# Value products one head later in a sparse-attention loop, its compressed branch behind the third head, and two tails in another order

## The chip, the cores and the metric

The kernel runs on one core of a Trainium2 chip. The metric is the time of one execution in device microseconds (us). TensorE is called PE in the rows (its weight loads PEld), VectorE DVE, ScalarE ACT, GpSimd POOL, and SyncE, which issues the transfers, SP.

## The reference

A trunk of two decoder layers on 256 tokens of width 1024, in float32. Each layer is a half feed-forward block, a token mixer and another half feed-forward block, each added to the residual. The mixer of layer 0 is native sparse attention, that of layer 1 differential attention.

```
for layer in range(2):
    x = x + 0.5 * swiglu(rmsnorm(x, ffn1_norm[layer]), ffn1_w_in[layer], ffn1_w_out[layer])
    hn = rmsnorm(x, mix_norm[layer])
    if layer == 0: y = nsa_mixer(hn, ...)
    else:          y = diff_mixer(hn, ...)
    x = x + y
    x = x + 0.5 * swiglu(rmsnorm(x, ffn2_norm[layer]), ffn2_w_in[layer], ffn2_w_out[layer])
```

Sparse attention has 16 query heads of 64 that share 4 key and value heads, and three branches: one over 15 compressed blocks, whose keys and values come out of a small MLP; one over selected blocks (with 256 tokens all that are causal); and one over a window.

```
o_cmp = softmax(q kc * scale - slope * dist) vc        # kc, vc = MLP of overlapping blocks
o_sel, o_win = the same over ks, vs and over kw, vw
o = g0 * o_cmp + g1 * o_sel + g2 * o_win               # g = sigmoid(gates), for each head
y = o @ w_out
```

Differential attention subtracts two softmaxes of each of 8 heads, multiplies by v, normalizes each head's output (subln) and projects it.

## The kernel before

Every product of full precision is made of three in a reduced one: weights and activations are split into a high and a low part (`whi`, `wlo`, `oh`, `ol`: ACT writes the high one, DVE subtracts it), and the products high by high, low by high and high by low are added up in one of eight PSUM banks, `B[0]` to `B[7]` (L383 to L385). The weights come in by DMA in an order fixed ahead and are split by L86 (ACT) and L89 (DVE).

The program's order on each engine is set by a scheduler out of the order in which the code issues, of the dependencies and of priorities: what stands inside `tc.high_priority` goes ahead of other work that is ready. Each engine then runs its own list in order. A piece of code that is written as a generator (`yield`) is advanced by its caller with `next` or finished with `run`.

Sparse attention (`nsa`) runs in these steps:

1. The projections. During the first (`q0`) and the one for v the generator `mlp` makes the compressed keys and values. Its last step, reached at `k == 4` of the v projection (`MLP_K`), turns the keys (transpose L748) and spreads the values (L750) in the bank `pk = B[4]`; ACT and DVE take them into `kcT` (L753, L754) and `vb` (L759).
2. `cmp_group(g, bank)`, the compressed branch for eight heads: 16 score products (L828), a softmax on DVE (L834 to L850, the exponential on ACT, L845), two transposes (L854) and the copy `pcT` (L855). For the first eight heads it is run before the loop, in `B[3]`; for the others it is part of the filler.
3. `head_loop` over 16 heads, written below. `qk(i)` are the scores (L894 and L897, high and low keys), `chain(i)` the softmax on DVE and ACT (L572, L573), the reciprocal and gating (L917, L918) and the scaling of the probabilities `p` (L921, L923), `tr(i)` six transposes (L930) and two copies `pT` (ACT L932, DVE L933). `pv(i)` does nothing for an even head; for an odd one it multiplies a pair's probabilities by the values: one product of the compressed branch (L942) and 16 half-height ones (L949), and then `oh` on ACT (L951) and `ol` on DVE (L952). Each pair of heads writes its half of `B[7]`.
4. `fill` advances the filler between the heads: the projection `q1` of the second eight heads, its transposes (`q_t`, L788, L791), the second `cmp_group`, and the part of the output projection (`out_proj`) for the pairs that are done. What is left of it is run behind the loop.

```
    def head_loop(n, qk, chain, tr, pv, fill, counts, pumps, mid=None, depth=1):
        for i in range(depth):
            qk(i)
            chain(i)
        if mid:
            mid(0)
        for i in range(n):
            with tc.high_priority(offset=0):
                tr(i)
                if i + depth < n:
                    qk(i + depth)
                    chain(i + depth)
            W.pump(pumps[i] // 10, 512)
            fill(counts[i])
            W.pump(pumps[i] % 10, 512)
            with tc.high_priority(offset=0):
                if mid and i + 1 < n:
                    mid(i + 1)
                pv(i)
```

The sparse loop calls it with a depth of 2 and no `mid`. `out_proj(half, 1, ...)` makes the second half of the heads for two of the four output banks: it yields after each bank's first products, and each bank's end is followed by the addition to the residual.

Differential attention ends with `sub_b(3, B[5])`, the normalization of the last two heads: a chain on DVE, four transposes (L1035), then `oh` on ACT (L1037) and `ol` on DVE (L1038), which the last products of each output bank need.

Of the kernel before, what the change touches and what calls it, by code (L numbers as in the profile page):

```python
# [25 lines left out]
HQ = 16  # L26
# [30 lines left out]
class Stream:  # L57
# [54 lines left out]
    def next(self, key):  # L112
        i = self.i
        assert self.chunks[i][0] == key, (self.chunks[i][0], key)
        while self.ns <= i:
            self._piece(2048)
        self.i += 1
        if self.eager:
            self.pump(99, 512)
        return self.split.pop(i)  # L120
# [3 lines left out]
def trunk_kernel(ctx, tc, x, ffn1_norm, ffn1_w_in, ffn1_w_out, mix_norm, ffn2_norm, ffn2_w_in, ffn2_w_out,  # L124
# [11 lines left out]
    B = [pp.tile([P, 512], F32, name=f"bank{i}") for i in range(8)]  # L136
# [438 lines left out]
    def out_proj(half, hg, oh, ol, nxt, scale):  # L575
        hi, lo = W.next("op%d%d" % (half, hg))
        hv, lv = halves(hi, 4), halves(lo, 4)
        for jp in range(2):
            for dd in range(4):
                d = half * 4 + dd  # L580
                for j in (2 * jp, 2 * jp + 1):
                    mm3(B[d // 2][:, (d % 2) * S:(d % 2 + 1) * S], hv[:, j, dd * P:(dd + 1) * P], lv[:, j, dd * P:(dd + 1) * P],
                        oh[:, 4 * hg + j, :], ol[:, 4 * hg + j, :], hg == 0 and j == 0 and d % 2 == 0, hg == 1 and j == 3)
                if hg == 1 and jp == 1 and d % 2:
                    residual_bank(d // 2, scale, nxt)
                if dd % 2:
                    yield

    def run(gen):
        for _ in gen:  # L590
            pass
# [10 lines left out]
                    self.live = False  # L602
                n -= 1

    def head_loop(n, qk, chain, tr, pv, fill, counts, pumps, mid=None, depth=1):
        for i in range(depth):
            qk(i)
            chain(i)
        if mid:
            mid(0)  # L610
        for i in range(n):
            with tc.high_priority(offset=0):
                tr(i)
                if i + depth < n:
                    qk(i + depth)
                    chain(i + depth)
            W.pump(pumps[i] // 10, 512)
            fill(counts[i])
            W.pump(pumps[i] % 10, 512)
            with tc.high_priority(offset=0):  # L620
                if mid and i + 1 < n:
                    mid(i + 1)
                pv(i)

    OWN_BANK = 5
    NSA_FILL = [7, 1, 1, 3, 0, 2, 2, 0, 0, 1, 0, 3, 0, 3, 0, 5]
    NSA_PUMP = [2, 42, 12, 42, 0, 24, 44, 40, 11, 42, 0, 4, 33, 3, 1, 40]
# [3 lines left out]
    NSA_POST = 0  # L631
    DIFF_POST = 0
    FFN_SPLIT = 0
    MLP_K = [0, 1, 4]
    QT_K = [1, 4, 5, 6]
    START_SPLIT = 0
    QRAW = 'svss'
# [5 lines left out]
    def nsa(nrm, nxt_g):  # L643
# [52 lines left out]
        def mlp():  # L696
            e2 = t2("e2", 64)
            nc.gpsimd.tensor_tensor(e2, ident[:, :64], ident[:, 64:], op=ALU.add)
            for kv in range(2):
                for half in range(2):  # L700
                    hi, lo = W.next("w1")
                    hv, lv = halves(hi, 8), halves(lo, 8)
                    for ii in range(8):
                        i = half * 8 + ii
# [37 lines left out]
            for g in range(2):  # L742
                for a in range(2):
                    c0 = (2 * g + a) * NCMP
                    nc.gpsimd.tensor_copy(halves(rr[:DH, g * P + a * DH:g * P + (a + 1) * DH], 4),
                                          ident[:DH, c0:c0 + NCMP].unsqueeze(1).to_broadcast([DH, 4, NCMP]))
            pk = B[4]
            nc.tensor.transpose(pk[:, :DH], ck[:DH], ident[:DH, :DH])  # L748
            for g in range(2):
                nc.tensor.matmul(pk[:, (1 + g) * DH:(2 + g) * DH], rr[:DH, g * P:(g + 1) * P], cc[:DH, DH:P],  # L750
# [12 lines left out]
        m = mlp()  # L763
# [44 lines left out]
        for tb in range(2):  # L808
            nc.scalar.activation(vn[:, tb, 0:256], B[2][:, tb * 256:(tb + 1) * 256], AF.Copy, scale=r[:, tb:tb + 1])
            nc.scalar.activation(vn[:, tb, 256:512], B[3 + 4 * tb][:, 0:256], AF.Copy, scale=r[:, tb:tb + 1])  # L810
        gv = gate.rearrange("p b (h c) -> p b h c", c=3)
        fcg = bp.tile([P, 2, HQ], F32, tag="fcg", name=nm("fcg"))
        oh = t8("oh", F32R).rearrange("p (k t) -> p k t", k=KT)
        ol = t8("ol", F32R).rearrange("p (k t) -> p k t", k=KT)
# [137 lines left out]
            nc.vector.tensor_tensor(ol[:, hp, :], b, oh[:, hp, :].bitcast(F32), op=ALU.subtract)  # L952

        gates()
        run(cmp_group(0, B[3]))
        fill = Fill(filler())
        W.eager = False
        W.pool = NSA_SPLIT
        head_loop(HQ, qk, chain, tr, pv, fill, NSA_FILL, NSA_PUMP, depth=2)
        W.eager = True  # L960
        W.pool = NSA_POST
        fill(1000)
        nxt = Norm(nxt_g)
        run(out_proj(0, 1, oh, ol, nxt, 1.0))
        run(out_proj(1, 1, oh, ol, nxt, 1.0))
        return nxt

    def diff(nrm, nxt_g):
# [5 lines left out]
        oh = t8("oh", F32R).rearrange("p (k t) -> p k t", k=KT)  # L974
# [67 lines left out]
        def pv(j, pt):  # L1042

            for h in (2 * j, 2 * j + 1):
                assert h in ready
                vs = slice(h * P, (h + 1) * P)
                a = (h % 2) * 256
                nc.tensor.matmul(pt[:, a:a + P], at[:, h % 5, :P], vt[:, 0, vs], start=True, stop=True, skip_group_check=True)
                for sb in range(2):
                    nc.tensor.matmul(pt[:, a + P:a + 2 * P], at[:, h % 5, (1 + sb) * P:(2 + sb) * P], vt[:, sb, vs],  # L1050
                                     start=sb == 0, stop=sb == 1, skip_group_check=True)
            raw = ob[j] = t2("oraw")
            nc.vector.tensor_copy(raw, pt)
# [126 lines left out]
        W.pool = TAIL_SPLIT  # L1180
        fill(1000)
        nxt = Norm(nxt_g)
        o1 = out_proj(0, 1, oh, ol, nxt, 1.0)
        next(o1)
        next(o1)
        W.pool = DIFF_POST
        run(s3)
        run(o1)
        run(out_proj(1, 1, oh, ol, nxt, 1.0))
        return nxt  # L1190

    W.pool = START_SPLIT
# [57 lines left out]
```

## Time and profile before

| | us |
|---|---|
| median of 3 runs | 1046.07 (1044.92 to 1046.37) |
| the profiled execution | 1046.42 |
| its span | 1044.6 |
| PE busy | 1027.9, 98% |
| DVE busy | 780.4, 75% |
| ACT busy | 621.1, 59% |
| POOL busy | 42.9, 4% |

The span is the time that the hardware profiler saw between the first and the last instruction of the core; the execution's time is that and what lies around it. Busy time is the sum over an engine's instructions of the time in which one was running; matmuls are pipelined, so two can overlap.

### The profile page before, as it was taken

What the parts mean: (1) busy time and instruction counts of PE and PEld (TensorE: products, weight loads), DVE (VectorE), ACT (ScalarE), POOL (GpSimd) and SP (SyncE); (2) the same over time, 40 slices, a digit from 0 to 9 for tenths busy, and PEclk for the clock granted to TensorE, in tenths of its full rate; (3) what the DMA queues carried; (4) which work ended last, traced back from release to release, by engine and by line L of the source; (5) the groups of instructions that cost most, each with busy time, mean ns of one, the idle gap of its engine ahead of it and who ended that gap; (6) DMA issues with size and microseconds to landing.
All of it is one profiled execution on the core that took longest, in us unless ns stands there. A gap on an engine that the chain in (4) does not pass through costs nothing.

```text
span 1044.6 us, 17571 instructions
## 1 busy us (share of the span) xinstructions
PE 1027.9 (98%) x6486; PEld 912.8 (87%) x6486; DVE 780.4 (75%) x1834; ACT 621.1 (59%) x1407; POOL 42.9 (4%) x86
## 2 busy tenths in 40 slices
PE   8999999999999999999999999999999999999998
PEld 7999999879777899999999999999878898888887
DVE  7775766889887795766679676667987988676674
ACT  6555555768677664555556555546677656556552
POOL 0000000000231100000000000000032000000000
PEclk9999999999999999999999999999999999999999
DMA  8656565478410256565555556565534335655541
GB/s 279 226 179 211 171 204 176 148 161 252 160 41 1 85 201 215 171 211 168 202 183 181 194 169 202 162 202 163 205 122 161 122 121 176 218 174 199 198 165 40
DMA packets 130482, 178.14 MB, mean 171 GB/s; under 512 B 5674, under 2 KB 105180, under 8 KB 130396
## 3 DMA queue, kind: packets, MB, share of 16 engines
q1 hardware_dynamic: 130220, 176.95, 52.3%
q8 instruction: 50, 0.82, 0.3%
q14 instruction: 36, 0.29, 0.1%
q10 hardware_dynamic: 176, 0.07, 0.0%
HBM read 175.96 MB, written 1.05 MB: 169 GB/s over the span
## 4 chain that ended last, share of the span: by engine, by line
PE 91%; DVE 4%; ACT 3%; issue 1%; DMA 1%; SPq 0%; POOL 0%; ACTq 0%; DVEq 0%; POOLq 0%
PE bank L420 28%; PE bank L422 15%; PE bank L383 7%; PE bank L385 7%; PE bank L384 7%; PE bank L388 6%; PE bank L389 6%; PE bank L390 6%; PE bank L949 2%; DVE wlo L89 2%; PE bank L930 1%; PE bank L897 1%; PE bank L1108 1%; ACT whi L86 1%; ACT p L573 1%
## 5 line engine op out<-in xcount | busy, mean ns | idle before, releaser
L89 DVE TENSOR_TENSOR wlo<-raw,whi 128x512 fp32r<-128x512 f32 x667 | 431.5, 683 | 136.0 <-ACT whi L86 134.6
L86 ACT CAST whi<-raw 128x512 fp32r<-128x512 f32 x667 | 373.5, 617 | 212.8 <-PE bank L420 126.3
L420 PE MATMUL bank<-xhl,whi 128*128 128x512 f32 x1280 | 450.8, 393 | 0.0
L422 PE MATMUL bank<-xhl,wlo 128*128 128x256 f32 x1280 | 361.7, 283 | 0.0
L420 PEld LDWEIGHTS bank<-xhl,whi 128*128 128x128 f32 x1280 | 240.5, 188 | 53.9
L422 PEld LDWEIGHTS bank<-xhl,wlo 128*128 128x128 f32 x1280 | 240.7, 188 | 0.4
L388 PE MATMUL bank<-hh,whi 128*128 128x256 f32 x528 | 149.4, 283 | 0.0
L389 PE MATMUL bank<-hh,wlo 128*128 128x256 f32 x528 | 149.3, 283 | 0.0
L390 PE MATMUL bank<-hl,whi 128*128 128x256 f32 x528 | 149.3, 283 | 0.0
L440 DVE TENSOR_TENSOR ab<-bank,sh 128x256 f32<-128x256 f32 x160 | 60.4, 418 | 73.7 <-ACT sh L439 73.7
L439 ACT COPY sh<-bank 128x256 f32<-128x256 f32 x160 | 55.9, 373 | 95.3 <-PE bank L422 95.1
L388 PEld LDWEIGHTS bank<-hh,whi 128*128 128x128 f32 x528 | 101.0, 191 | 1.2
L390 PEld LDWEIGHTS bank<-hl,whi 128*128 128x128 f32 x528 | 101.1, 191 | 0.0
L389 PEld LDWEIGHTS bank<-hh,wlo 128*128 128x128 f32 x528 | 101.0, 191 | 0.0
L383 PE MATMUL bank<-whi,xhl 128*128 128x512 f32 (+2 forms) x192 | 75.7, 394 | 0.0
L384 PE MATMUL bank<-wlo,xhl 128*128 128x512 f32 (+2 forms) x192 | 72.9, 380 | 0.7 <-DVE wlo L89 0.7
L385 PE MATMUL bank<-whi,xhl 128*128 128x512 f32 (+2 forms) x192 | 72.9, 380 | 0.0
L442 DVE TENSOR_TENSOR ab<-ab,rb 128x512 f32<-128x512 f32 x80 | 54.6, 683 | 0.0
L573 ACT ACTIVATE p<-p,mn 128x128 f32<-128x128 f32 (+1 forms) x96 | 43.1, 452 | 11.9 <-DVE mn L572 11.5
L448 ACT CAST hh<-sh 128x256 fp32r<-128x256 f32 x88 | 34.8, 399 | 19.4 <-DVE sh L446 19.4
L384 PEld LDWEIGHTS bank<-wlo,xhl 128*128 128x128 f32 x192 | 36.2, 189 | 6.9 <-DVE wlo L89 1.1
L385 PEld LDWEIGHTS bank<-whi,xhl 128*128 128x128 f32 x192 | 36.1, 188 | 6.7
(259 smaller groups left out, 1331.0 us busy)
## 6 DMA issues: line engine op xcount, KB each, us to landing
raw<-in_ffn_w_in_dram SPq DMA_DIRECT2D x174, 512.0 KB, 5.0
raw<-in_ffn_w_out_dram SPq DMA_DIRECT2D x44, 1024.0 KB, 5.0
raw<-in_diff_w_in_dram SPq DMA_DIRECT2D x12, 1024.0 KB, 5.1
raw<-in_nsa_w_in_dram SPq DMA_DIRECT2D x6, 1024.0 KB, 6.1
raw<-in_nsa_cmp_w_dram SPq DMA_DIRECT2D x8, 512.0 KB, 5.1
raw<-in_nsa_w_out_dram SPq DMA_DIRECT2D x4, 1024.0 KB
raw<-in_diff_w_out_dram SPq DMA_DIRECT2D x4, 1024.0 KB
raw<-in_nsa_w_in_dram SPq DMA_DIRECT2D x4, 512.0 KB
```

What stands on the lines that cost most here:

```text
L86: self.nc.scalar.copy(hi[:, a:b], raw[:, a:b])
L89: self.nc.vector.tensor_tensor(lo[:, a:m], raw[:, a:m], hi[:, a:m].bitcast(F32), op=ALU.subtract)
L383: nc.tensor.matmul(ps, wh, xh, start=start, stop=False, skip_group_check=True)
L384: nc.tensor.matmul(ps, wh, xl, start=False, stop=False, skip_group_check=True)
L385: nc.tensor.matmul(ps, wl, xh, start=False, stop=stop, skip_group_check=True)
L388: nc.tensor.matmul(ps, wh, xh, start=start, stop=False, skip_group_check=True)
L389: nc.tensor.matmul(ps, wl, xh, start=False, stop=False, skip_group_check=True)
L390: nc.tensor.matmul(ps, wh, xl, start=False, stop=stop, skip_group_check=True)
L420: nc.tensor.matmul(g, wh, nrm.both[:, k].rearrange("p c t -> p (c t)"), start=k == 0, stop=False, skip_group_check=True)
L422: nc.tensor.matmul(g[:, :S], wl, nrm.hi[:, k, :], start=False, stop=k == KT - 1, skip_group_check=True)
L439: nc.scalar.copy(sh[j][:, cs], g[:, S:])
L440: nc.vector.tensor_tensor(ab[j][:, cs], g[:, :S], sh[j][:, cs], op=ALU.add)
```

## The change

`head_loop` issues the value products of head i-1 behind the transposes of head i, with high priority, in place of those of head i at the end of its turn; those of the last head are issued in the tail, behind the first products of the output projection's first bank. The compressed branch of the first eight heads is no longer run before the loop but in its first turn (`once`), in `B[7]`. By then the scores of heads 0 to 2 have been issued. The last step of `mlp` is run behind the evictions of the v projection in place of at `k == 4`, in `B[7]`. In both tails the first products of all four output banks are issued before the last ones of any.

```diff
-    def head_loop(n, qk, chain, tr, pv, fill, counts, pumps, mid=None, depth=1):
+    def head_loop(n, qk, chain, tr, pv, fill, counts, pumps, depth, once):
         for i in range(depth):
             qk(i)
             chain(i)
-        if mid:
-            mid(0)
         for i in range(n):
             with tc.high_priority(offset=0):
                 tr(i)
+                if i:
+                    pv(i - 1)
                 if i + depth < n:
                     qk(i + depth)
                     chain(i + depth)
+            if i == 0:
+                once()
             W.pump(pumps[i] // 10, 512)
             fill(counts[i])
             W.pump(pumps[i] % 10, 512)
-            with tc.high_priority(offset=0):
-                if mid and i + 1 < n:
-                    mid(i + 1)
-                pv(i)
...
-    MLP_K = [0, 1, 4]
+    MLP_K = [0, 1]
...
-            pk = B[4]
+            pk = B[7]
...
+        run(m)
...
         gates()
-        run(cmp_group(0, B[3]))
         fill = Fill(filler())
...
-        head_loop(HQ, qk, chain, tr, pv, fill, NSA_FILL, NSA_PUMP, depth=2)
+        head_loop(HQ, qk, chain, tr, pv, fill, NSA_FILL, NSA_PUMP, 2, lambda: run(cmp_group(0, B[7])))
...
-        run(out_proj(0, 1, oh, ol, nxt, 1.0))
-        run(out_proj(1, 1, oh, ol, nxt, 1.0))
+        o = [out_proj(half, 1, oh, ol, nxt, 1.0) for half in range(2)]
+        next(o[0])
+        pv(HQ - 1)
+        next(o[0])
+        next(o[1])
+        next(o[1])
+        run(o[0])
+        run(o[1])
...
-        o1 = out_proj(0, 1, oh, ol, nxt, 1.0)
-        next(o1)
-        next(o1)
+        o = [out_proj(half, 1, oh, ol, nxt, 1.0) for half in range(2)]
+        for i in range(4):
+            next(o[i // 2])
         W.pool = DIFF_POST
         run(s3)
-        run(o1)
-        run(out_proj(1, 1, oh, ol, nxt, 1.0))
+        run(o[0])
+        run(o[1])
```

In the kernel after, the lines of `nsa` stand one or two earlier (L930 is L929 there, L942 L941, L949 L948, L788 L786, L828 L827, L894 L893, L897 L896, L854 L853, L839 L838, L847 L846, L917 L916, L918 L917, L923 L922, L933 L932, L780 L778), and L1035 is L1039. In the following lists of instructions in program order, bank_82 to bank_89 are `B[0]` to `B[7]`, and a number behind a name tells tiles of one name apart.

PE before, from the end of head 0's transposes to the first value products:

```order
L788 MATMUL bank_83<-cst,qhl_3189 128x128 x2
L897 MATMUL bank_88<-kTh_2450,qT_2669 128x512
L897 MATMUL bank_88<-kTl_2451,qT_2669 128x512
L788 MATMUL bank_82<-cst,qhl_3189 128x128 x4
L949 MATMUL bank_89<-pT_3012,vn_2899 64x256
L788 MATMUL bank_83<-cst,qhl_3189 128x128 x4
L828 MATMUL bank_82<-kcT_2452,qT_2669 128x32
```

PE after, from the transposes of head 1 (p_2951) to the first q transposes (L786):

```order
L929 MATMUL bank_84<-cst,p_2951 128x128 x4
L929 MATMUL bank_85<-cst,p_2951 128x128 x2
L896 MATMUL bank_87<-kTh_2450,qT_2669 128x512
L896 MATMUL bank_87<-kTl_2451,qT_2669 128x512
L929 MATMUL bank_85<-cst,p_2984 128x128 x2
L929 MATMUL bank_84<-cst,p_2984 128x128 x4
L893 MATMUL bank_86<-kTh_2450,qT_2669 128x256
L893 MATMUL bank_86<-kTl_2451,qT_2669 128x256
L853 MATMUL bank_89<-cst,csc_3018 128x128 x2
...
L941 MATMUL bank_89<-pcT_3035,vb_2906 128x256
L948 MATMUL bank_89<-pT_2975,vn_2886 64x256
...
L786 MATMUL bank_82<-cst,qhl_3189 128x128
```

The q transposes of the second group and its compressed scores stood ahead of and around the first value products; now they stand behind the first L941, which reads pcT.

DVE before, the compressed branch (csc, cmn, cf) and the first scores of head 0 (p_2964):

```order
L839 TENSOR_TENSOR csc_2937<-bank_85,csc_2937 128x256
...
L844 TENSOR_TENSOR csc_2937<-cmn_2945,csc_2937 128x256
L847 TENSOR_REDUCE cf_2949<-csc_2937 128x16
L572 ISA p_2964,mn_2965<-bank_86,bias_2912,fac_2667 128x128
```

DVE after, the same branch among the scaling of head 2 (p_2984) and the weight splits L89:

```order
L89 TENSOR_TENSOR wlo_3452<-raw_2855,whi_3451 128x512
L838 TENSOR_TENSOR csc_3018<-bank_89,csc_3018 128x256
L917 TENSOR_TENSOR f_2995<-f_2995,gate_2887 128x4
L89 TENSOR_TENSOR wlo_3452<-raw_2855,whi_3451 128x512
...
L843 TENSOR_TENSOR csc_3018<-cmn_3026,csc_3018 128x256
L89 TENSOR_TENSOR wlo_3452<-raw_2855,whi_3451 128x512
L846 TENSOR_REDUCE cf_3030<-csc_3018 128x16
L572 ISA p_3102,mn_3103<-bank_86,bias_2912,fac_2667 128x128
```

The branch stood ahead of head 0's first score step; now it stands behind the score steps of heads 0, 1 and 2, ahead of head 3's (p_3102).

PE before, a block of value products late in the loop, between scores and the output projection:

```order
L894 MATMUL bank_86<-kTl_2451,qT_2669 128x256
L949 MATMUL bank_89<-pT_3636,vn_2899 64x256
L949 MATMUL bank_89<-pT_3603,vn_2899 64x128
L949 MATMUL bank_89<-pT_3636,vn_2899 64x128
...
L949 MATMUL bank_89<-pT_3636,vn_2899 64x128
L384 MATMUL bank_85<-ol_2911,whi_3126 128x256
```

PE after, the value products of the same pair:

```order
L948 MATMUL bank_89<-pT_3592,vn_2886 64x256
L893 MATMUL bank_86<-kTh_2450,qT_2669 128x256
L893 MATMUL bank_86<-kTl_2451,qT_2669 128x256
L383 MATMUL bank_84<-oh_2910,whi_3126 128x256
L948 MATMUL bank_89<-pT_3636,vn_2886 64x256
L384 MATMUL bank_84<-ol_2911,whi_3126 128x256
L948 MATMUL bank_89<-pT_3592,vn_2886 64x128
L385 MATMUL bank_84<-oh_2910,wlo_3127 128x256
L948 MATMUL bank_89<-pT_3636,vn_2886 64x128
```

What stood in one block now alternates with scores and with products of the output projection. From the third L942 to the end of the loop there are 18 blocks of L949 before and 25 of L948 after.

PE before, the tail of differential attention (on is the normalized output of the last heads):

```order
L385 MATMUL bank_83<-oh_7972,wlo_8893 128x256
L1035 MATMUL bank_87<-cst,on_9006 128x128 x4
L384 MATMUL bank_84<-ol_7973,whi_9014 128x256
...
L384 MATMUL bank_84<-ol_7973,whi_9014 128x256
L383 MATMUL bank_82<-oh_7972,whi_8892 128x256
```

PE after, the same place:

```order
L385 MATMUL bank_85<-oh_7972,wlo_9015 128x256
L1039 MATMUL bank_87<-cst,on_9006 128x128 x4
L383 MATMUL bank_82<-oh_7972,whi_8892 128x256
L383 MATMUL bank_83<-oh_7972,whi_8892 128x256
L383 MATMUL bank_84<-oh_7972,whi_9014 128x256
L383 MATMUL bank_85<-oh_7972,whi_9014 128x256
```

Seven products of bank_84 that need only earlier heads stood behind the transposes; now all of these stand ahead, and the four that need the transposed heads follow directly.

## Rows read from the trace of the kernel before

**Rows 1.** The page: span, and busy time of each engine.

```profile
span 1044.6 us, 17571 instructions
...
PE 1027.9 (98%) x6486; PEld 912.8 (87%) x6486; DVE 780.4 (75%) x1834; ACT 621.1 (59%) x1407; POOL 42.9 (4%) x86
```

**Rows 2.** Busy time by stage; columns PE, PEld, DVE, ACT, POOL, clock, DMA, GB/s.

```profile
262.50:303.30 40.80, 37.51 (x219) 28.46 (x218) 36.60 (x142) 27.88 (x88) 11.03 (x21) 0.96 0.31 104
303.30:360.40 57.10, 56.66 (x394) 43.96 (x393) 42.83 (x176) 38.26 (x125) 12.64 (x22) 1.00 0.15 46
281.00:284.30 3.30, 3.30 (x12) 2.36 (x12) 3.10 (x14) 3.30 (x13) 1.01 (x2) 0.50 0.09 26
```

**Rows 3.** PE's timeline to 302: start, duration, line, count [idle before, releaser].

```profile
272.75 1.85 PE L828 MATMUL bank<-kcT,qT 128*128 128x32 f32 x16
...
279.55 0.39 PE L894 MATMUL bank<-kTh,qT 128*128 128x256 f32 x1 [1.10 <-DVE mn L572]
...
280.47 0.41 PE L854 MATMUL bank<-cst,csc 128*128 128x128 f32 x2 [0.42 <-ACT p L573]
...
284.71 0.49 PE L930 MATMUL bank<-cst,p 128*128 128x128 f32 x3
...
297.76 1.51 PE L949 MATMUL bank<-pT,vn 128*64 128x256 f32 x14 [0.46 <-ACT pT L932]
299.73 0.39 PE L383 MATMUL bank<-oh,whi 128*128 128x256 f32 x1 [0.46 <-ACT oh L951]
...
301.56 0.38 PE L383 MATMUL bank<-oh,whi 128*128 128x256 f32 x1 [0.49 <-ACT pT L932]
```

**Rows 4.** DVE's timeline of the same stretch.

```profile
272.22 1.27 DVE L759 TENSOR_TENSOR vb<-bank,cst 128x512 f32<-128x512 f32 x2
...
278.46 0.42 DVE L847 TENSOR_REDUCE cf<-csc 128x16 f32<-128x256 f32 x1 [0.54 <-ACT csc L845]
278.80 0.34 DVE L572 CUSTOM_DVE_ANT_0 p<-bank,bias,fac 128x128 f32<-128x128 f32 x1
...
302.70 0.41 DVE L952 TENSOR_TENSOR ol<-bank,oh 128x256 fp32r<-128x256 f32 x1
```

**Rows 5.** DVE's groups by line and form, 279.9 to 303.1: busy us, mean ns.

```profile
L572 DVE CUSTOM_DVE_ANT_0 p<-bank,bias,fac 128x256 f32<-128x256 f32 x12 | 5.4, 476 | 0.0
L572 DVE CUSTOM_DVE_ANT_0 p<-bank,bias,fac 128x128 f32<-128x128 f32 x10 | 3.4, 340 | 0.0
L89 DVE TENSOR_TENSOR wlo<-raw,whi 128x512 fp32r<-128x512 f32 x4 | 2.7, 698 | 0.0
...
L933 DVE COPY pT<-bank 128x256 f32<-128x256 f32 x5 | 2.1, 420 | 0.8 <-PE bank L930 0.7
```

**Rows 6.** PE's timeline at the third L942 and two blocks of value products.

```profile
303.32 0.60 PE L942 MATMUL bank<-pcT,vb 128*128 128x256 f32 x2
303.85 0.65 PE L949 MATMUL bank<-pT,vn 128*64 128x256 f32 x2
304.43 0.39 PE L384 MATMUL bank<-ol,whi 128*128 128x256 f32 x1
304.65 0.28 PE L385 MATMUL bank<-oh,wlo 128*128 128x256 f32 x1
304.77 0.28 PE L383 MATMUL bank<-oh,whi 128*128 128x256 f32 x1
...
307.53 1.51 PE L949 MATMUL bank<-pT,vn 128*64 128x256 f32 x14
308.97 0.39 PE L383 MATMUL bank<-oh,whi 128*128 128x256 f32 x1
```

**Rows 7.** PE's timeline in the tail of differential attention.

```profile
838.59 0.62 PE L383 MATMUL bank<-oh,whi 128*128 128x256 f32 x3 [0.78 <-ACT oh L1037]
839.38 0.39 PE L383 MATMUL bank<-oh,whi 128*128 128x256 f32 x1 [0.17 <-DVE ol L1038]
...
844.99 0.60 PE L1035 MATMUL bank<-cst,on 128*128 128x128 f32 x4
```

## Prediction

> **What bounds the kernel now.** I began with the page's first lines: TensorE (PE) is busy for 98% of a span of 1044.6 us [rows 1]. So what PE waits, and what its instructions cost it, is the time; another engine counts only where PE waits for it. Next I cut the sparse-attention stage in two with the table by stage [rows 2]. From 262.5 to 303.3 PE is busy for 37.51 of 40.80 us, 3.29 idle, while VectorE (DVE) is busy for 36.60: here the two bind together. From 303.3 to 360.4 PE is busy for 56.66 of 57.10 us, so nearly nothing is to be won there, and every extra cost on PE is paid in full. The clock stands beside it: 0.96 in the first part, 1.00 in the second; from 281.0 to 284.3 it is 0.50 (1.2 GHz), 3.3 us in which PE does half as much, so 1.65 lost. What PE did before: it had waited 1.10 us for a row minimum of DVE at 279.55 and 0.42 us for ScalarE (ACT) at 280.47 [rows 3].
>
> The timeline of PE shows where the idle time lies: besides those two, 0.46, 0.46 and 0.49 us at 297.76, 299.73 and 301.56 [rows 3]. DVE's timeline shows why head 0 is late: its scores are ready, but DVE reads them (L572) only at 278.80, behind the compressed branch's chain, which ends there with the reduce of 278.46 [rows 4]. Head 0's transposes end at 285.2 [rows 3].
>
> **The change, part by part.**
>
> *The compressed branch behind head 2, the front of the loop.* DVE need not do the compressed branch first. It is free for head 0 when the second of the L759 pair ends, 272.22 + 1.27 = 273.5, against 278.80 [rows 4]: 5.3 us earlier, so head 0's transposes end near 279.9. Then the order turns against it. The changed order of PE has, between those transposes and the first value product, only the scores of heads 2 to 5, two heads' transposes and two small transposes. At the spacings of [rows 3] and the means of [rows 5] for their partners on DVE I count this as 3.4 us of PE work (an estimate). The value product needs pcT, the end of the compressed branch; the 16 q transposes and 16 compressed scores of the second group, which filled PE here before, now stand behind it. How long DVE needs: each instruction starts some 0.07 before its predecessor ends (278.46 + 0.42 against 278.80 [rows 4]), so I take 0.07 off each mean of [rows 5]. Ahead of csc's last step stand in the changed order: two L933 copies 0.7, two L780 at the mean of L89 1.3, four 128-wide score steps 1.1, three 256-wide ones 1.2 plus their accumulator reads, 0.4 (an estimate), five scalings priced like the 128-wide score step 1.4, three weight splits (L89) 1.9, four small ones 0.4; and the branch itself, seven steps of 0.35 and four small ones, 3.0. Sum 11.4, so from 279.9 to about 291.3. PE idles some 8 of these 11 us, more than the 3.29 it idled in the whole part before. The first value products then end near 294.3, with 3.6 us of q transposes and compressed scores still to do (in before the same were done by 290.7: 272.75 shows 16 compressed scores at 1.85 us [rows 3], and the 16 transposes take about as long). The work of DVE up to the second split of the attention output (302.70 [rows 4]) is the same set in both, plus 0.1, and its idle time moves rather than goes, so I put that row 1 us later, and the third L942, which follows it at 303.32 before [rows 6], at about 304.8: **+1.5**. Bounds: if all idle time of PE in this part went, -3.3 [rows 2]; if PE's late 3.6 us came wholly on top and nothing hid it, +4.
>
> *Clock.* Before, waits of 1.10 and 0.42 us were followed by 3.3 us at 0.50 [rows 2, 3]. The new waits are longer, several in a row, so I expect some 2.4 us more at 0.50, half of it lost: **+1.2**. Bounds: -1.65 (none left) and +2.9 (9 us at 0.50 in place of 3.3).
>
> *Value products one head later.* In before a pair's value products mostly stand as one block on PE, because they are issued when their transposes have just been copied and everything else is behind them. Issued behind the next head's transposes, they become ready among other work, and the scheduler deals them out. Counted in the order from the third L942 on: 18 blocks of L949 before, 25 after, for the same products. What a block costs: two products that stand alone take 0.58 (303.85 to 304.43), while fourteen in a row take 1.44 (307.53 to 308.97), 0.103 each [rows 6]. So two alone cost 0.58 - 0.21 = 0.37 over their share; and the product behind them starts its successor 0.22 later (304.43 to 304.65), where 0.12 is usual (304.65 to 304.77) [rows 6]: 0.10 more. Together 0.47 a block. Seven more blocks: **+3.3**. Lower bound: a larger block's own start is partly hidden by what runs before it; at 0.16 a block (a guess of a third) 1.1.
>
> The Trainium skill speaks against this part as well: "TensorEngine Tiling (Array Packing)", Key Properties, says that changing the tiling mode drains TensorE, and these products use 64 of 128 output partitions where their neighbours use all. This case's rows agree in kind, 0.47 us a block [rows 6]. From "TensorE: Matmul & The Clock Gate", the part of a single warm product's latency that isn't its columns, 398 cycles at 2.4 GHz or 0.166 us, twice a block, would make 7 x 0.33 = 2.3 us in place of 3.3, an estimate.
>
> *Waits that go.* Products issued a head later find their copies ready. From 303.3 on all waits of PE sum to 0.44 [rows 2]: **-0.4**, at most. The waits of ahead (297.76) are in the front's term.
>
> *Last head's value products behind the first half of the output projection.* Their copy and split on ACT and DVE (two steps of some 0.4, 302.70 [rows 4]) are hidden by the 36 first-half products still to come, 36 x 0.12 = 4.3 us [rows 6]: 0. If that cover were gone, 0.8.
>
> *The keys' last products in another bank.* PE does the same products, later, behind the evictions of v: some 0.9 us of PE work in the same stage, nothing waits for it but the compressed branch, which now comes later: 0. Without cover 0.5.
>
> *Tails.* In differential attention the last transposes (L1035) stand at 844.99 with seven products that don't need them right behind, and no wait follows [rows 7]. Afterwards all 48 first-half products stand ahead of them and four products that need their result directly behind. That is the place that the trace has at 838.59 and 839.38: after the same transposes PE waited 0.78 us for ACT's oh and 0.17 us for DVE's ol [rows 7]. 0.95 and some 0.15 for starting again: **+1.1** (bounds 0.8 and 1.4). In the sparse tail the first residual bank comes later and the last at the same place: 0; what follows needs all four.
>
> *Sum.* 1.5 + 1.2 + 3.3 - 0.4 + 1.1 = +6.7. The profiled execution took 1046.42 us, 0.35 above the median of the runs shown, so 1053.1 as profiled and **1052.8** against the median.
>
> **Rivals.**
>
> *The front gains (faster).* Heads that start 5.3 us earlier keep PE supplied, and the value products issued late wait for nothing: all 3.29 idle and the 1.65 of the slow clock go, -4.9. With the blocks at their lower bound and the tail: -4.9 + 1.1 - 0.4 + 1.1 = -3.1, 1043.0. For it: DVE's chain in front of head 0 is the visible wait at 279.55. Against: only 3.4 us of PE work stand in 11 us of DVE work. It decides if the third L942 starts before about 299.5.
>
> *The gains and the blocks cancel (no change).* The same front, but the blocks at 3.3: -4.9 + 3.3 - 0.4 + 1.1 = -0.9, 1045.2; or a front that comes out even, with blocks that fall into waits of PE, and only the tail left, 1047.2.
>
> *The clock stays low longer (slower still).* If PE's bursts of 291 to 300 all run at 0.50, 9 us in place of the 5.7 assumed: +1.65, 1054.5; with the front at its bound of +4, 1057.
>
> The Trainium skill ("TensorE: Matmul & The Clock Gate", HAM oscillation) tells of kernels whose short bursts between waits each start at the low clock; the 0.50 behind the waits of 279.55 agrees [rows 2, 3], and that is the case of this rival.
>
> **How the numbers follow.** My forecast has a chance of 0.50, with a range of its own of 1050 to 1056; the low clock 0.15; the cancelling case 0.18; the gaining front 0.17. A difference of 0.2% is about what a measurement of this kernel can tell from none: 1044.0 and 1048.2. So faster 0.17, same 0.18, slower 0.65. The range, 1044 to 1057, leaves out the gaining front and little else.
>
> **What would show it.** Right: head 0's transposes end before 281; PE is idle for most of 281 to 291 with DVE as the releaser of the first L941; a longer stretch at 0.50; the third L941 after 303.3; single and double L948 entries in the timeline between products of the output projection, and a PE busy time of L948 some microseconds up; behind the last L1039 a wait for ACT's oh near 0.8. Wrong: a third L941 before 300, a clock of 1.00 throughout, or L948 blocks that cost their neighbours nothing.

## The result, and the profile after

The changed kernel takes 1053.64 us (median of 4 runs, 1051.43 to 1054.74), the kernel before 1046.22 us beside it: a ratio of 1.0066 with a 95% interval of 1.0051 to 1.0080, some 6.9 us slower (5.3 to 8.4 by the interval; the two medians are 7.4 apart). The prediction was 1052.8.

First the page of the kernel after, answering to [rows 1]: span, and busy time of each engine.

```profile
span 1052.8 us, 17566 instructions
...
PE 1033.1 (98%) x6486; PEld 915.6 (87%) x6486; DVE 779.9 (74%) x1834; ACT 621.5 (59%) x1407; POOL 44.3 (4%) x86
```

The span is 8.2 us longer, and PE's busy time 5.2 us of that: more than half of the loss looks like work. No product was added, so these are instructions that took longer. Three stretches hold nearly all of it. They begin and end with the same instructions in each kernel: the *front* from the last keys' transpose (L748 before) to the third pair's compressed product (L942 before), the *rest* from there to the first feed-forward product behind the sparse tail, and the *tail* of differential attention from the transposes of the second last group of heads to its end. Busy time by stage (columns as in [rows 2]), before:

```profile
270.62:303.32 32.70, 29.41 (x179) 22.38 (x179) 28.96 (x117) 23.17 (x76) 8.20 (x15) 0.95 0.22 74
303.32:360.44 57.12, 56.67 (x395) 43.98 (x394) 42.85 (x176) 38.30 (x126) 12.64 (x22) 1.00 0.15 46
837.16:854.15 16.99, 16.05 (x129) 15.45 (x129) 12.05 (x28) 8.67 (x17) 0.00 (x0) 1.00 0.32 109
```

and after:

```profile
270.61:306.51 35.90, 29.59 (x175) 22.22 (x175) 29.46 (x123) 24.25 (x77) 9.01 (x16) 0.86 0.23 78
306.51:365.70 59.19, 58.98 (x398) 45.18 (x397) 42.36 (x169) 38.91 (x126) 12.92 (x22) 1.00 0.12 37
842.74:862.34 19.60, 17.83 (x128) 16.95 (x129) 10.49 (x24) 7.11 (x14) 0.00 (x0) 0.91 0.29 95
```

So +3.2, +2.1 and +2.6 us, 7.9 of the 8.2. In the front PE's idle time doubles, from 3.29 to 6.31 us. In the rest there is hardly any idle time in either kernel: PE works longer. In the tail both the wait and the clock change.

**The front.** PE's timeline after, answering to [rows 3]: start, duration, line, count, and in brackets the idle time ahead and what ended it.

```profile
281.94 0.39 PE L893 MATMUL bank<-kTh,qT 128*128 128x256 f32 x1 [1.44 <-DVE mn L572]
...
287.35 0.90 PE L929 MATMUL bank<-cst,p 128*128 128x128 f32 x3 [3.33 <-POOL p L922]
288.65 0.90 PE L929 MATMUL bank<-cst,p 128*128 128x128 f32 x3 [0.40 <-DVE p L922]
290.57 0.58 PE L893 MATMUL bank<-kTh,qT 128*128 128x256 f32 x1 [1.01 <-DVE mn L572]
...
293.80 2.56 PE L948 MATMUL bank<-pT,vn 128*64 128x256 f32 x16
```

Four waits, 6.2 us, stand ahead of the first value products, and those run at the slow clock (16 in 2.56 us). DVE and ACT in the same stretch, answering to [rows 4]:

```profile
273.55 0.34 DVE L572 CUSTOM_DVE_ANT_0 p<-bank,bias,fac 128x128 f32<-128x128 f32 x1
...
280.06 0.42 DVE L932 COPY pT<-bank 128x256 f32<-128x256 f32 x1 [1.73 <-PE bank L929]
...
285.85 0.42 DVE L838 TENSOR_TENSOR csc<-bank,csc 128x256 f32<-128x256 f32 x1 [0.65 <-POOL csc L835]
...
290.92 0.42 DVE L849 TENSOR_TENSOR csc<-csc,cf 128x256 f32<-128x256 f32 x1
```

```profile
292.18 0.37 ACT L854 COPY pcT<-bank 128x256 f32<-128x256 f32 x1 [0.54 <-PE bank L853]
...
292.95 1.08 ACT L550 ACTIVATE qsq<-bank 128x512 f32<-128x512 f32 x2
```

Head 0 is read at 273.55, 5.25 us earlier than before, as worked out. Then DVE is the bound: from head 0's copy to the end of the branch's last step it takes 280.06 to 291.34, and in these 11.28 us it is busy for 10.47, PE for 5.09. And there is something that the prediction had not seen: the square L550 on ACT reads the banks into which the q transposes go. It ran at 281.99 before and at 292.95 now, since ACT's order has it behind pcT:

```profile
281.99 1.08 ACT L550 ACTIVATE qsq<-bank 128x512 f32<-128x512 f32 x2
```

So with ACT's order as it is, no order of PE could have filled PE's idle time with the q transposes.

**The rest.** A pair's value products late in the loop, answering to [rows 6]:

```profile
338.26 0.65 PE L948 MATMUL bank<-pT,vn 128*64 128x256 f32 x2
338.84 0.38 PE L384 MATMUL bank<-ol,whi 128*128 128x256 f32 x1
339.15 0.43 PE L948 MATMUL bank<-pT,vn 128*64 128x128 f32 x2
339.51 0.39 PE L385 MATMUL bank<-oh,wlo 128*128 128x256 f32 x1
339.83 0.86 PE L948 MATMUL bank<-pT,vn 128*64 128x128 f32 x6
340.63 0.38 PE L383 MATMUL bank<-oh,whi 128*128 128x256 f32 x1
```

Each starts the next one late: a product of the output projection between two blocks has 0.31 us from its start to that of the next block (338.84 to 339.15), where 0.12 is usual [rows 6]. The profile shows no wait in these rows; the time is in the instructions.

**The tail.** Answering to [rows 7]:

```profile
842.74 0.66 PE L1039 MATMUL bank<-cst,on 128*128 128x128 f32 x4 [0.74 <-DVE on L1036]
844.17 0.62 PE L383 MATMUL bank<-oh,whi 128*128 128x256 f32 x3 [0.78 <-ACT oh L1041]
844.96 0.39 PE L383 MATMUL bank<-oh,whi 128*128 128x256 f32 x1 [0.17 <-DVE ol L1042]
...
845.98 0.41 PE L383 MATMUL bank<-oh,whi 128*128 128x256 f32 x1
846.19 0.41 PE L384 MATMUL bank<-ol,whi 128*128 128x256 f32 x1
...
854.81 0.60 PE L1039 MATMUL bank<-cst,on 128*128 128x128 f32 x4
856.19 0.74 PE L383 MATMUL bank<-oh,whi 128*128 128x256 f32 x4 [0.78 <-ACT oh L1041]
```

The first three rows are those of before, waits and all: they belong to the group of heads ahead of the last one. New are the wait of 0.78 us at 856.19, behind the last transposes, and products 0.21 us apart in place of 0.12 around 846: the clock. By stage, after:

```profile
286.00:287.50 1.50, 0.15 (x1) 0.15 (x2) 1.50 (x6) 0.36 (x1) 0.76 (x1) 0.50 0.00 0
287.50:292.00 4.50, 2.96 (x11) 1.84 (x12) 4.50 (x20) 2.41 (x8) 0.46 (x2) 0.50 0.00 0
292.80:296.00 3.20, 3.20 (x17) 1.81 (x18) 2.23 (x13) 2.38 (x9) 1.26 (x3) 0.51 0.62 193
845.50:848.70 3.20, 3.20 (x17) 3.20 (x16) 2.17 (x10) 0.00 (x0) 0.00 (x0) 0.50 0.00 0
```

In the front some 10 us at 0.50 (1.2 GHz), where before had 3.3 [rows 2]; in the tail 3.2 us, where before had none behind the same waits.

### The profile page after: what moved, and what is told of

Its sections match the earlier page's. It is cut to its first block, busy times and chain, and to the rows that moved or that the text cites. A ratio compares the mean times of both kernels' runs of the same rounds, so it can differ in the third digit from the quotient of the medians.

```text
span 1052.8 us, 17566 instructions
## 1 busy us (share of the span) xinstructions
PE 1033.1 (98%) x6486; PEld 915.6 (87%) x6486; DVE 779.9 (74%) x1834; ACT 621.5 (59%) x1407; POOL 44.3 (4%) x86
## 4 chain that ended last, share of the span: by engine, by line
PE 89%; DVE 5%; ACT 3%; DMA 1%; issue 1%; POOL 0%; SPq 0%; ACTq 0%; DVEq 0%; POOLq 0%
PE bank L420 27%; PE bank L422 14%; PE bank L384 7%; PE bank L383 7%; PE bank L385 7%; PE bank L390 6%; PE bank L388 6%; PE bank L389 6%; DVE wlo L89 2%; PE bank L948 2%; PE bank L929 1%; DMA raw<-in_ffn_w_in_dram 1%; PE bank L1112 1%; ACT whi L86 1%; PE bank L896 1%
## 5 line engine op out<-in xcount | busy, mean ns | idle before, releaser
L89 DVE TENSOR_TENSOR wlo<-raw,whi 128x512 fp32r<-128x512 f32 x667 | 432.6, 686 | 135.9 <-ACT whi L86 135.4
```

What stands on the lines that cost most here:

```text
L89: self.nc.vector.tensor_tensor(lo[:, a:m], raw[:, a:m], hi[:, a:m].bitcast(F32), op=ALU.subtract)
```

## The experiments

The theory: the three parts add. The branch behind three softmaxes starves PE (front), the later value products are dealt out in more blocks (rest), and the last transposes lose their cover (tail). The rivals: the tails carry the loss; the blocks are free and only waits shift; GpSimd or the clock is the cause. Each experiment was timed against the kernel before on its own chip (ratio, 95% interval); front, rest and tail are read from its trace as above, so that they can be compared one by one.

| kernel | ratio to before (interval) | front | rest | tail |
|---|---|---|---|---|
| before | 1 | 32.70 | 57.12 | 16.99 |
| after | 1.0066 (1.0051 to 1.0080) | 35.90 | 59.19 | 19.60 |
| loop alone | 1.0069 (1.0057 to 1.0082) | 35.91 | 59.66 | 18.47 |
| differential tail alone | 1.0013 (1.0004 to 1.0022) | 32.54 | 57.13 | 19.61 |
| branch late alone | 1.0033 (1.0021 to 1.0045) | 37.23 | 56.71 | 18.39 |
| value products late alone | 1.0023 (1.0013 to 1.0033) | 29.91 | 62.40 | 16.98 |
| late keys and sparse tail alone | 1.0003 (0.9994 to 1.0012) | 32.36 | 57.09 | 16.97 |
| after, head 2 without GpSimd | 1.0068 (1.0055 to 1.0082) | 36.08 | 59.16 | 18.13 |
| after, sections | 1.0160 (1.0142 to 1.0178) | 38.88 | 66.36 | 18.12 |
| before, sections | 1.0165 (1.0148 to 1.0183) | 31.39 | 75.46 | 18.48 |
| value products late, priority | 1.0006 (0.9997 to 1.0016) | 29.62 | 61.25 | 16.99 |
| after, priority | 1.0047 (1.0034 to 1.0060) | 31.97 | 60.48 | 18.14 |
| after, transposes behind three banks | 1.0040 (1.0027 to 1.0053) | 35.41 | 59.17 | 18.42 |
| branch behind head 0, priority | 1.0021 (1.0009 to 1.0033) | 30.44 | 61.76 | 18.46 |

Where the value products are issued at another place, the third pair's compressed product moves against the work around it, so there front and rest are compared as a sum: 89.82 before.

**The loop alone.** After, with both tails of before.

```diff
         nxt = Norm(nxt_g)
-        o = [out_proj(half, 1, oh, ol, nxt, 1.0) for half in range(2)]
...
+        pv(HQ - 1)
+        run(out_proj(0, 1, oh, ol, nxt, 1.0))
+        run(out_proj(1, 1, oh, ol, nxt, 1.0))
```

> The changed loop, compressed branch and bank, but both tails in their old order (the last head's value products ahead of the tail). Theory (the parts add: front of the loop +3.2 us and split value products +2.1 us as read from the trace of after, tail of differential attention +1.1 us and more where the clock falls there): +5.3 us against before, 2 to 2.6 us less than the whole change. Rival (the tails carry the loss, the loop only shifts waits): under +2 us.

7.2 us slower (1.0057 to 1.0082), and front and rest 5.75 us longer in the trace: the loop carries the loss. The rival under 2 us falls. The 2 us less than the whole change that were expected are not seen: either interval is over 2 us wide, and this trace has the slow clock in its tail too (18.47), with the old order there. The rest is 0.47 us longer than in after, so the new order of the sparse tail may be worth something behind the changed loop; that was not followed up.

**The tail alone.**

```diff
-        next(o1)
-        next(o1)
+        for i in range(4):
+            next(o[i // 2])
```

> The kernel before with the tail of differential attention alone in the new order. Theory: the last four transposes lose their cover, a wait of 0.78 us for ACT's oh and some 0.3 us of restarting behind them: +1.1 us. Rival one: the waits of this tail bring down the clock, as the trace of after shows it at 0.50 from 845.4 to 848.8: +2.6 us. Rival two: the wait is hidden: 0.

1.4 us slower (0.4 to 2.3), as the theory has it; the first rival's 2.6 lies above the interval. Its trace shows the wait of 0.78 us behind the last transposes, and here the clock too: a tail of 19.61, 2.6 us over before, as the first rival has it. The execution with the trace (1048.62 us) is the slowest of twelve. And it shows a second thing: its front is instruction for instruction that of before, with the same waits of 1.10 and 0.42 us, but at a clock of 1.00 throughout.

```profile
270.21:302.75 32.54, 28.44 (x179) 21.31 (x179) 28.87 (x117) 23.16 (x76) 8.20 (x15) 1.00 0.22 74
```

So the two fronts differ by 0.16 us, where 3.3 us at 0.50 had been priced at 1.65: PE's busy time is 0.97 us less here, but its idle time 0.81 us more. At the full clock PE waits where it had been slow before, for instance for the square on ACT ahead of the q transposes:

```profile
282.22 0.93 PE L788 MATMUL bank<-cst,qhl 128*128 128x128 f32 x6 [0.29 <-ACT qsq L550]
```

**The branch late alone.**

```diff
-        run(cmp_group(0, B[3]))
...
+            if i == 0:
+                mid()
```

Here `mid` runs `cmp_group(0, B[7])`; the value products stay at the end of their turn, and the keys' last products are late as in after.

> The kernel before with the compressed branch behind the third head (and the keys' last products late, in the other bank), but the value products at the end of their own head's turn and the old tails; its order has 18 blocks of value products from the third pair on, as before. Theory: the branch's place alone makes the loss of the front: the third pair's compressed product 3.2 us later than in before, PE idle for some 6 us between 280 and 292 and a clock of 0.50 behind it; +3.2 us. Rival: the loss comes from the value products that stand ahead of the q transposes a head later; without them the early heads gain: 0 or -1 us.

3.5 us slower (2.2 to 4.7), front and rest 4.1 us longer, with waits of 1.45, 2.98, 0.40 and 1.01 us and 13 us at 0.50 in the front. The branch's place makes the front's loss without the late value products (the late keys, which stand in this run too, cost nothing by the run of the small parts further down); the rival, for which the late value products were needed, falls.

**The value products late alone.**

```diff
                 tr(i)
+                if i:
+                    pv(i - 1)
...
-                pv(i)
...
+        pv(HQ - 1)
```

> The kernel before with the value products one head later alone (compressed branch before the loop, old bank, old tails); its order has 25 blocks of value products from the third pair on, as after, and the front nearly as before. Theory: seven more blocks at 0.3 to 0.47 us less some 0.4 us of waits that go: +2 to +3 us, and no stretch at 0.50 longer than that of before. Rival: the blocks fall into times in which PE waits, the waits of 297 to 302 go: -1 to 0 us.

2.4 us slower (1.4 to 3.5); front and rest together 92.31, 2.5 us more. PE's idle time in both together did not fall (3.73 us before, 4.05 here). The busy time of the value products alone (columns PE, PEld, clock, DMA, GB/s), before and here:

```profile
270.62:360.44 89.82, 19.02 (x128) 9.66 (x128) 0.98 0.17 56
```

```profile
271.28:363.59 92.31, 21.60 (x128) 10.12 (x128) 0.98 0.17 54
```

2.58 us more for seven more blocks, 0.37 a block, where 0.47 had been assumed for a block and its neighbour. All of it lies behind the third pair, at a clock of 1.00 in both (14.48 before, 17.06 here and also in after).

**The small parts: late keys, and the sparse tail's order.**

```diff
-    MLP_K = [0, 1, 4]
+    MLP_K = [0, 1]
...
-            pk = B[4]
+            pk = B[7]
...
+        for i in range(4):
+            next(o[i // 2])
```

> The kernel before with the two small parts alone: the keys' last products behind the evictions of v and in the other bank, and the sparse tail with the first products of all four output banks ahead of the last ones. Its order has the value products in 18 blocks from the third pair on, as before. Theory: both are covered, 0 us (within 0.5). Rival: the later keys delay the compressed branch, which DVE does first here, and with it all heads: +0.5 to +1.5 us.

No difference (-0.6 to +1.3 us), and the three stretches are as before within 0.34 us. Both are covered.

**Head 2 without GpSimd.**

```diff
-'vvvp'
+'vvvv'
```

> The kernel after with the one scaling of head 2 that GpSimd does (behind the branch's distances on its queue) given to VectorE. In the trace of after PE waits 3.33 us for it ahead of head 2's transposes. Theory (DVE's chain of branch, scalings and weight splits bounds the front, GpSimd is only the last of several to end): the named wait goes to DVE's scalings and to the value products behind, no gain, 0 to -0.5 us against after, and the third pair's compressed product still 3 us later than in before. Rival (GpSimd's queue is the cause): -1.5 to -3 us against after.

1.0068 against after's 1.0066: no gain. The wait goes where the theory puts it, from GpSimd to DVE:

```profile
285.77 0.45 PE L929 MATMUL bank<-cst,p 128*128 128x128 f32 x1 [3.60 <-DVE p L922]
```

A releaser is only the last of those that were late. Its tail, with the order of after and no slow clock, is 18.13: 1.14 us more than before, the price of the lost cover by itself. The other 1.47 us, up to after's 19.60, are the clock, since the instructions and waits of the two tails are the same.

**Held together by sections, after and before.**

```diff
+            with tc.tile_critical():
                 for br in range(2):
...
```

> The kernel after with the 16 value products of each pair held together in the order (a critical section): 8 blocks in place of 30. The section brings a jump and an empty instruction at either side of each block on PE. Theory (splitting costs 0.3 us and more a block): at least 2 us faster than after, as much as 5. Rival (the blocks' price is small and the time was lost in the front alone): within 1 us of after, or slower by what the 16 jumps cost.

> The kernel before with the value products of each pair held together in the same way: 8 blocks in place of 23. Theory: 15 blocks fewer at 0.2 to 0.4 us, less what the jumps cost: 1 to 4 us faster than before. Rival: the jumps and the waits at the head of each block take it back: no change or slower.

Both 17 us slower, so nothing can be concluded on the blocks: by the trace the section waits at its head for more than its inputs. In before with sections the third pair's block waits 2.33 us, and the last pair's 4.17, for a transfer of feed-forward weights that it doesn't read; in after with sections the first pair's block waits 4.19 us for such a transfer and the others 0.43 to 0.69 us each. In after these waits are about half of the idle time that PE gained (21.4 us in front and rest, 6.5 without sections); the other half was not followed up.

```profile
311.44 2.83 PE L950 MATMUL bank<-pT,vn 128*64 128x256 f32 x16 [2.33 <-DMA raw<-in_ffn_w_in_dram]
```

This trace, like the next row (the second pair in after with sections), has the 16 products in a row. Here they ran at 0.50, there at 1.00, so the row gives their price at the full clock, 1.52 us:

```profile
306.58 1.52 PE L949 MATMUL bank<-pT,vn 128*64 128x256 f32 x16 [0.48 <-DVE ss L551]
```

**Held together by priority.** The value products late, alone and in after, with a priority above all other work.

```diff
                 if i:
-                    pv(i - 1)
+                    with tc.high_priority(offset=1000):
+                        pv(i - 1)
```

> The kernel with the value products one head later alone (as the earlier run of that), but with a higher priority for them than for all else: the order has them in 20 blocks, 16 of them from the third pair on, in place of 30 and 25. Theory (a block costs 0.3 to 0.47 us): 10 blocks fewer, -3 to -4.5 us against that run, so 1 to 2.5 us below the kernel before. Rival (lateness itself, not the blocks, costs): within 1 us of that run, so still 1.5 to 3 us above before.

> The kernel after with the same higher priority for the value products: 18 blocks, 15 of them from the third pair on, in place of 30 and 25; the front and both tails as in after. Theory: 12 blocks fewer, 10 of them behind the third pair: -3 to -5 us against after, and the front still 3 us late. Rival: within 1 us of after.

Late alone: 1.0006 in place of 1.0023, some 1.8 us won, and no longer told from before (-0.3 to +1.7 us), where 1 to 2.5 us below it was expected. After: 1.0047 in place of 1.0066, some 2 us, where 3 to 5 were expected. In both pairs the intervals overlap; in the traces front and rest together are 1.44 us (92.31 to 90.87) and 2.64 us (95.09 to 92.45) shorter. The theory's sign is right, its size is not. The front of after keeps its four waits (1.44, 3.33, 0.63 and 1.01 us); its 31.97 in the table is short because the third pair's product stands earlier in the work. The value products themselves gave back what was expected, late alone:

```profile
270.42:361.29 90.87, 18.16 (x128) 9.84 (x128) 1.00 0.17 56
```

3.44 us less for ten blocks fewer, 0.34 a block. In the rest, PE's whole busy time fell by more (61.24 to 56.60 us, of which 3.22 are the value products); why the other products took 1.4 us less is open. But new waits took much of it (PE's idle time in the rest is 4.65 us, 61.25 - 56.60, in place of 1.16): with the value products pulled to the front, the block of the fourth pair waits for its copy, and later transposes for DVE.

```profile
315.54 0.87 PE L948 MATMUL bank<-pT,vn 128*64 128x256 f32 x8 [2.17 <-ACT pT L931]
...
351.86 0.44 PE L929 MATMUL bank<-cst,p 128*128 128x128 f32 x2 [1.57 <-DVE p L922]
```

**The last transposes behind three banks.** After, with `run(s3)` behind the third bank's first products.

> The kernel after with the last four transposes of differential attention behind the first products of three output banks in place of four: the fourth bank's 12 products, 1.4 us, stand behind them. Theory (the lost cover makes the wait of 0.78 us and the restart): the wait for ACT's oh is gone and the time is 1.1 us below after. Rival (that tail's cost is the clock): no change beyond 0.3 us.

The wait for oh is gone: behind the transposes run the twelve products of the fourth bank.

```profile
853.10 0.60 PE L1039 MATMUL bank<-cst,on 128*128 128x128 f32 x4
853.45 0.36 PE L383 MATMUL bank<-oh,whi 128*128 128x256 f32 x1
```

1.0040, some 2.7 us under after's ratio; the intervals of the two overlap, so the size is not settled, but the trace bears out 1.1: the tail is 18.42 with the slow clock in it, 1.18 less than after's with the slow clock.

Its front, which is after's in every instruction, shows what the clock costs there. The first value products start 23.19 us into the front in both traces, behind four waits that end at the same places. Here the clock rises within them, sooner than in after (2.56 us at 293.80):

```profile
294.32 2.07 PE L948 MATMUL bank<-pT,vn 128*64 128x256 f32 x16
```

The 0.49 us saved are still there at the end of the front (35.41 against 35.90), and the rest is the same.

**The branch behind head 0.** With the priority and the old tail of differential attention.

```diff
             chain(i)
+            if i == 0:
+                once()
...
-            if i == 0:
-                once()
```

> Value products one head later with the higher priority (19 blocks, 15 from the third pair on), both tails of before in differential attention, and the compressed branch behind the first head alone: between before the loop (the run of the value products alone with that priority: from the third-pair view, front and rest of the stage 90.9 us together, before 89.8) and behind the third (92.5 us, in the run of after with that priority). Theory (every softmax that VectorE does ahead of the branch delays the first value products and what queues on PE behind them): in between, 91 to 92 us for front and rest, 1 to 2 us slower than before. Rival (what costs is only the third head's scaling and GpSimd in the branch's way; behind one head VectorE is free early and the branch still is in time): below 89.5 us and faster than before by 0.5 to 2 us.

2.2 us slower than before (0.9 to 3.5), front and rest 92.20: between 90.87 (ahead of the loop) and 92.45 (behind head 2), near the latter. The rival falls. How much the second and third softmax add is open: by these sums nearly nothing, but in the ratios this run stands between the other two (1.0006, 1.0021 and 1.0047; some 1.1 us of the last are its tail). The clock differs too: this front has some 6.5 us at 0.50, the one with the branch ahead of the loop none, and of the 1.33 us between the two 0.99 are PE's busy time and only 0.34 waits.

## Why the prediction was right

Its sum was 6.7 us, the measured difference is some 6.9. The parts add: timed alone, branch, value products and tail come to 3.5 + 2.4 + 1.4 = 7.3. That the sum is as near as 0.2 us is in part luck: in the trace the front is 0.5 above its terms and the rest 0.8 below. Against the median of after, 1053.64, the forecast (1052.8) and the rival in which the clock stays low (1054.5) are equally far off, and the clock did stay low as long as that rival says (some 10 us in the front, where it has 9). By its steps:

- **The front** was put at 1.5 for the starved PE and 1.2 for the clock, 2.7 together; measured 3.2 in the trace, 3.5 with the branch late alone. DVE's work to the end of the branch was put at 279.9 to 291.3 and took 280.06 to 291.34. PE's work in that time was put at 3.4 us and its idle time at 8; they are 5.09, part of it at the slow clock, and 6.2. The reasoning of the clock's term failed: an engine that waits anyway loses little to a slow clock, so before's front was only 0.16 us longer than the same front at 1.00, and not the 1.65 from which the term was made. The clock was also low for longer than predicted, 10 us in place of 5.7. What it costs in after lies behind 292.8, where PE has no wait: 16 value products take 2.56 us there and 1.52 at the full clock, the pair of L941 ahead of them 0.99 from start to start and 0.53 in the third pair. That is 1.5 us of the 3.2, an estimate from these rows, of which the run with the transposes behind three banks shows 0.49 by itself. What is left, some 1.7 us, is put down to the starved PE. So the two terms came out near their sizes, the clock's for another reason than the one given. The reason given for the delayed q transposes, that they stand behind the first value products, is not the whole one: the square on ACT held their banks until 294.0. That is read from the traces and was not tried by moving the square.
- **The blocks** were put at 3.3 and the waits that go at -0.4. Measured: 0.34 to 0.37 a block in the value products' busy time, 2.4 to 2.6 us for seven, and +2.1 us for the rest in after (PE's busy time +2.3, its waits 0.45 to 0.21, so -0.2 of the -0.4). The mechanism is shown both ways (seven blocks more, ten fewer); the term was mis-sized by a fifth to a third. Of the 0.47, the 0.37 that two products cost over their share came out as put. The 0.10 that the product behind a block loses did not show in the sum: PE's busy time in the rest without the value products is 42.19 us before and 41.92 after. The size of the blocks isn't the reason, since those of two products rose from 10 to 18 (counted in the two traces from the third pair on). The Trainium skill ("TensorEngine Tiling (Array Packing)", Key Properties) has changing the tiling mode drain TensorE. The traces agree in kind, at 0.34 to 0.37 us a block, and show no drain as such. The 0.33 a block was an estimate from the latency that the Trainium skill gives for a single bf16 product ("TensorE: Matmul & The Clock Gate", section Single matmul latency). The traces come close to it, for products of another type.
- **The last transposes** were put at 1.1; 1.14 in the trace without the slow clock, 1.4 (0.4 to 2.3) timed alone.
- **The small parts** were put at 0, and are.
- **The profiled execution** is 1.5 us worse than these parts say, by the tail's clock. That was not predicted, and nothing shows it to be the change's doing: the slow stretch of some 3 us in that tail stands in the traces of after, of the loop alone, of the branch late alone, of the new tail alone and of others, and not in those of before, of the value products alone or of head 2 without GpSimd. Old and new tails are on both sides.

The gaining front needed a third compressed product before 299.5; the value products alone had it at 301.2, with the priority at 300.0, and nothing was won: front and rest together took 92.31 and 90.87 us, against 89.82 before.

## What to carry to other kernels

Where two engines bind together, look for which of them a moved chain falls on: starting head 0 five microseconds earlier won nothing, because the same DVE work then stood ahead of the one result that every value product needs. Count in how many pieces a scheduler deals out instructions of another shape than their neighbours': here some 0.35 us a piece, without a wait to show for it, so that it is seen only in busy time. And give the last instructions that wait for another engine some independent work to run behind them; twelve products sufficed.

## What the runs showed of the hardware that was not expected

The granted clock of the same instructions behind the same waits differs from trace to trace. Behind 1.10 and 0.42 us of waiting the front of before ran 3.3 us at 0.50, and the same front with the new tail none. Behind some 0.74, 0.78 and 0.17 us in the tail, seven of the fourteen traces have some 3 us at 0.50, worth 1.5 us there, where PE is the bound. Runs of one kernel spread by some 3 us (1051.43 to 1054.74, 1044.92 to 1047.77); whether such stretches make that spread was not shown, since only one execution of each has a trace.
